# Mixer chains of a hybrid mLSTM and HGRN2 layer, their product groups spaced by the unit

## The chip, the cores and the metric

The kernel runs on one core of one Trainium2 chip. A core has TensorE (PE, matrix products into PSUM banks), VectorE (DVE), ScalarE (ACT), GpSimd (POOL) and SyncE (SP, which issues the DMAs). The metric is the time of one execution on the device in microseconds (us); lower is better.

## The reference

One decoder layer works on 1024 new prompt positions and 8 sequences of 4 sampled positions, 1056 columns in all. What matters here:

```python
p = jnp.einsum('btd,dp->btp', _rmsnorm(x, norm_mix), w_in) + b_in       # 1024 -> 4104
out_a = sigmoid(o) * headnorm(mlstm(silu(conv(qk)), v, i, f))           # 4 heads of 128
out_b = headnorm(hgrn(silu(q), f, i)) * silu(g)                         # 4 heads of 128
x = x + concat([out_a, out_b]) @ w_out
x = x + (silu(h2 @ w_gate) * (h2 @ w_up)) @ w_down
# mlstm: W = exp(D - m); num = w_inter * (q C) + ((q k) * W) v; C <- decay * C + sum(w_last k v)
# hgrn:  A = sum_k q k exp(b_t - b_s); o = (q exp(b)) S + A v; S <- exp(b_L) S + (k exp(b_L - b)) v
```

headnorm divides each head's row by the root of its mean square. The states C and S are outputs too.

## The kernel before, in words

All data lies transposed, features on the partitions and time along the columns. The 1056 columns are cut into three blocks b of 288, 384 and 384 (the first holds the 32 sampled columns). The in-projection takes one weight tile of 128 output features at a time; each **unit** is one weight tile times one block: eight k-tiles of three main matmuls each (L135 to L137: high part of x times high part of w, low times high, high times low). For a head h and a block b there are four units: q, k, v, o for the mLSTM heads (a), then f, q, v, g for the HGRN2 heads (b). After all heads comes the out-projection, again in units (264 columns), which needs all chains' outputs split into HI and LO (mix_split, L994 and L995).

The work between projections, the **mixer**, runs in Python generators: mix_a(h, b) and mix_b(h, b). A list of active chains is advanced by hook(), which is called after the second, fourth and sixth k-tile and after the end of each unit, so there are four **places** per unit and 16 per block of a head. At a place each active chain, oldest first, writes its next piece of instructions behind the main matmuls; yield n lets n places pass. So the queues of all engines are in the order in which hook() met the pieces, and the waits in the chains set which places share pieces. finish(key) calls hook() until a chain is done, at one place: that happens before the out-projection's unit needs a k-tile whose split isn't written.

A chain's pieces on PE: in mix_a scores, k transposed, v transposed (L528, L532, L535), state products (L551), output (L572, L574), and the output transposed (L590); in mix_b four groups of level products (L777 twice, then L855 and L860), v and k transposed (L874, L877), state products (L891), output (L911, L913), transposed output (L928). The numbers of places between them stand in MAW (L502, a row for h = 0 and each block, and one for all other heads) and, for mix_b, as constants in its yields. All of them write PSUM tiles of the tag mx, of which four rotate; main matmuls have three of the tag mm.

Between the groups other engines work: ACT squares the output (L580, L918), DVE and POOL take the root (norm_cols, L495 to L500), DVE multiplies by it (L585, L923), and after the transposes DVE multiplies by the gate (L592, L930) and writes the result to X, from where mix_split takes it. In mix_b DVE takes products into AD (L784), ACT copies them to AT (L846), and the steps (L796, L798, L804, ACT L801, L802) prepare q and k of the next level; AT times v is the output. The units' evacuations are ACT and DVE too: the HGRN2 gate by L743 to L746. A weight tile is split by ACT (L96) and by POOL (L97, 512 columns each). Sampled columns have a chain of their own (sample_core, L626 to L699), with state products L674 and L646 for each sequence.

Of the kernel before, what the change touches and what calls it, by code (L numbers as in the profile page):

```python
# [9 lines left out]
F32 = mybir.dt.float32  # L10
# [13 lines left out]
NB = 3  # L24
H = 4
# [15 lines left out]
def hybrid_step(ctx: ExitStack, tc: tile.TileContext, i, o):  # L41
# [6 lines left out]
    mp = p1.enter_context(tc.tile_pool(name="mixp", bufs=1))  # L48
# [3 lines left out]
    def bank(tag="mx"):  # L52
        return psum.tile([128, 512], F32, tag=tag, name=tag, bufs={"mm": 3, "mx": 4, "so": 1}[tag])
# [136 lines left out]

    def ntile(tag="nt"):
        if tag in ("raw", "W"):
            return mp.tile([128, 387], F32, tag=tag, name=tag, bufs=2 if tag == "raw" else 1)
        if tag == "na":
            return cn.tile([128, QN], F32, tag=tag, name=tag, bufs=1)
        return cn.tile([128, 384], F32, tag=tag, name=tag, bufs=2)
# [43 lines left out]
    def tl(tag, n=384, bufs=2, dt=F32, p=128):  # L240
        return mp.tile([p, n], dt, tag=tag, name=tag, bufs=bufs)
# [250 lines left out]
    def norm_cols(s, sqs, nch, d2=None, p=128):  # L492
# [14 lines left out]

    def mix_a(h, b):
        w = MAW[b if h == 0 else 3]
# [3 lines left out]
        while ("gc", b) not in done or ("cv", "k") not in done:  # L513
            yield 1
        ng, wi = S["ng", h, b], S["wi", h, b]
        W = mp.tile([128, 387], F32, tag="W", name="W", bufs=1)
        for c in range(ncb):
            s = slice(c * 128, c * 128 + 128)
            nc.vector.scalar_tensor_tensor(W[:, s], ng[:, s], cols[:, c0 + c, 0, h:h + 1], maskneg,
                                           op0=OP.add, op1=OP.add)  # L520
        nc.scalar.activation(W[:, :npr], W[:, :npr], AF.Exp)
        qw = tl("qw")
# [14 lines left out]
        if (h, b) == (0, 0):  # L537
            nc.gpsimd.memset(ktm, 0.0)
        kt = tl("kt", 384, 1)
# [5 lines left out]
                                cols[:, c0:c0 + ncb, 2, h:h + 1].to_broadcast([128, ncb, 128]), op=OP.mult)  # L545
        nc.vector.scalar_tensor_tensor(W[:, :npr], pS[:, :npr], QS, W[:, :npr], op0=OP.mult, op1=OP.mult)
        yield w[2]
# [22 lines left out]
        for c in range(ncb):  # L570
            s = slice(c * 128, c * 128 + 128)
            nc.tensor.matmul(pO[:, c, 0:129], W[:, s], vt[:, c, 0:129], start=True, stop=cin[c] is None)  # L572
            if cin[c] is not None:
                nc.tensor.matmul(pO[:, c, 0:129], qw[:, s], cin[c], start=False, stop=True)  # L574
        yield w[5]
        sm = mp.tile([128, 3, 4], F32, tag="sm", name="sm", bufs=2)
        hn = tl("kt", 384, 1)
        nc.scalar.activation(sm[:, 1, :ncb, None], pO[:, :ncb, 128:129], AF.Square)
        for c in range(ncb):
            nc.scalar.activation(hn[:, c * 128:c * 128 + 128], pO[:, c, 0:128], AF.Square, accum_out=sm[:, 0, c:c + 1])  # L580
# [121 lines left out]
    def sample_a():  # L702
# [12 lines left out]
        for h in range(H):  # L715
            nc.tensor.matmul(pS[32 * h:32 * h + 32, 0:32], kS[:, h, :], qS[:, h, :], start=True, stop=True,
                             tile_position=(0, 32 * h))
        W = tl("sW", 32, 1)
        nc.vector.scalar_tensor_tensor(W, ngS, scol[:, 0:1], mneg4, op0=OP.add, op1=OP.add)
# [29 lines left out]
    def mix_b(h, b):  # L749
# [2 lines left out]
        AT, AD = ATs[atn[0] % 2], ADs[atn[0] % 2]  # L752
        atn[0] += 1
        samp = b == 0
        gx = tl("wib", 388, 2)
        qp = tl("qw")

# [32 lines left out]
        def step(lv, src, dst):  # L790

            nn = n if samp and lv <= 2 else npr
            G, go = gst
            nb = nn // (2 * lv)
            gv = G[:, go:go + nn // lv].rearrange("p (n two) -> p n two", two=2)
            nc.vector.tensor_tensor(odd(dst[0][:, :nn], lv), odd(src[0][:, :nn], lv), gv[:, :, 0:1].to_broadcast([128, nb, lv]),  # L796
                                    op=OP.mult)
            nc.vector.tensor_tensor(even(dst[1][:, :nn], lv), even(src[1][:, :nn], lv), gv[:, :, 1:2].to_broadcast([128, nb, lv]),  # L798
                                    op=OP.mult)
            if dst is not src:  # L800
                nc.scalar.activation(even(dst[0][:, :nn], lv), even(src[0][:, :nn], lv), AF.Copy)  # L801
                nc.scalar.activation(odd(dst[1][:, :nn], lv), odd(src[1][:, :nn], lv), AF.Copy)  # L802
            go2 = 0 if lv == 1 else go + nn // lv
            nc.vector.tensor_tensor(gx[:, go2:go2 + nb, None], gv[:, :, 0:1], gv[:, :, 1:2], op=OP.mult)  # L804
            gst[:] = gx, go2
# [59 lines left out]
            nc.scalar.activation(AT[s0:s0 + 32, :ncb, s0 + 32:s0 + 64], pc[s0:s0 + 32], AF.Copy)  # L865
        nc.scalar.activation(AT[0:64, :ncb, 64:128], ps[0:64, 128:128 + 64 * ncb].rearrange("p (c t) -> p c t", t=64), AF.Copy)
        step(64, B, B)
        yield 1
        go, qp, k = gst[1], qB, kB
        v = S["vb", h, b]  # L870
        pK, pV = bank(), bank()
# [7 lines left out]
        kt = tl("kt", 384, 1)  # L879
# [3 lines left out]
        if samp:  # L883
            nc.gpsimd.tensor_copy(ss_["sv"][:, h, :], v[:, 256:288])
            nc.gpsimd.tensor_copy(ss_["so"][:, h, :], S["g", h, b][:, 256:288])
        yield 2
        pU = bank()
        C = mp.tile([128, 3, 130], F32, tag="C", name="C", bufs=2)
        for c in range(ncb):
# [14 lines left out]
        Sst[h] = prev  # L904
        if b == 2:
            nc.sync.dma_start(o["Sp"][h], prev)
        yield 2
        pO = bank()
        for c in range(ncb):
            s = slice(c * 128, c * 128 + 128)  # L910
# [2 lines left out]
                nc.tensor.matmul(pO[:, s], qp[:, s], cin[c], start=False, stop=True)  # L913
        yield 1
        sm = mp.tile([128, 3, 4], F32, tag="sm", name="sm", bufs=2)
        hn = tl("kt", 384, 1)
        for c in range(ncb):
            nc.scalar.activation(hn[:, c * 128:c * 128 + 128], pO[:, c * 128:c * 128 + 128], AF.Square,  # L918
                                 accum_out=sm[:, 0, c:c + 1])
# [1 line left out]
        yield 2  # L921
        for c in range(ncb):
            nc.vector.tensor_scalar_mul(hn[:, c * 128:c * 128 + 128], pO[:, c * 128:c * 128 + 128], sm[:, 2, c:c + 1])  # L923
        yield 6
        pH = bank()
        for c in range(ncb):
            s = slice(c * 128, c * 128 + 128)
# [23 lines left out]
    for h in range(H):  # L951
        ts = [wtile(wa[1 + 4 * h + j]) for j in range(4)]
        for b in range(NB):
            gu = len(units) + (1 if b else 0)
            evs = [conv_evac("q", h, b), conv_evac("k", h, b),
                   act_evac("v", "v", AF.Identity, V_BIN + 8 + h, h, b),
                   act_evac("o", "go", AF.Sigmoid, V_BIN + 12 + h, h, b, 2)]
            posts = [(lambda h, b: lambda: load_bc(h, b))(h, b) if h else None, None,
                     spawn((lambda h, b: lambda: mix_a(h, b))(h, b), "a", h, b), None]
            if h == H - 1 and b == 0:  # L960
                posts[3] = spawn(sample_a, "sa")
            in_group(ts, b, evs, posts, (("mm", "mm", "mx", "mx") if (h, b) == (0, 0) else None))
            if h == 0:
                unit(tg, hrhs(b), KT, gates_evac(b))
                units.insert(gu, units.pop())
# [43 lines left out]
    def out_evac(m, q):  # L1009
        def ev(ps):  # L1010
            x = xq(q)
            nc.vector.tensor_tensor(x[:, m, :], x[:, m, :], ps[:, :QN], op=OP.add)
            dst = ntile(("raw", "raw", "W", "na")[q]) if m == 0 else ntile()
            nc.scalar.activation(dst[:, :QN], x[:, m, :], AF.Square)
            if m == 0:
                naccs[q] = dst
            else:
                nc.vector.tensor_tensor(naccs[q][:, :QN], naccs[q][:, :QN], dst[:, :QN], op=OP.add)
            if m in (4, KT - 1):
                s = slice(0, 5) if m == 4 else slice(5, KT)  # L1020
                nc.sync.dma_start(d_x[:, s, q * QN:(q + 1) * QN], x[:, s, :])
            if m == KT - 1:
                start(norm2(q), ("n2", q))
        return ev
# [945 lines left out]
```

## Time and profile before

| what | value |
|---|---|
| time, median of 3 runs | 1389.78 us (1387.84 to 1392.84) |
| the profiled execution | 1390.61 us |
| its span, first to last instruction | 1388.5 us |
| PE busy | 1339.8 us, 96% |
| DVE, ACT, POOL busy | 865.7, 558.1, 595.9 us |
| mean granted clock of TensorE | 0.979 |

The profile lists busy time by engine, the waits of an instruction with the engine and tile that released it, and instructions in order of time. A matmul's listed duration overlaps the next one's, so the spacing of starts tells what one costs. In-projection and mixers fill the time to about 563 us, the out-projection follows, then the feed-forward network.

### The profile page before, as it was taken

Reading aid. Unit: us, or ns where it says so; the run is one execution under the profiler, and the core shown is the slowest. Engines: PE = TensorE matmul, PEld = TensorE weight load, DVE = VectorE, ACT = ScalarE, POOL = GpSimd, SP = SyncE. Lnnn points to the kernel's source line nnn. Section 1 sums busy time; section 2 is a strip of 40 time slices with the busy share of each in tenths; the row PEclk is TensorE's granted clock in tenths of the full one; section 3 lists DMA queues with packets and bytes.
Section 4 is the critical chain, followed back from the end, with each engine's and each line's share of the span. In section 5 each row is a group of like instructions: output and inputs, shape, how many; then the busy total and the mean of one; then the engine's idle time right before and its main releaser. Section 6 shows DMA issues by size and latency. Waiting matters only on the chain. (4 is left out here: it accounts for less than half of the span.)

```text
span 1388.5 us, 29405 instructions
## 1 busy us (share of the span) xinstructions
PE 1339.8 (96%) x11600; PEld 1309.3 (94%) x11600; DVE 865.7 (62%) x2060; ACT 558.1 (40%) x1315; POOL 595.9 (43%) x566
## 2 busy tenths in 40 slices
PE   7988999999999999999999999999999999999996
PEld 6878999899999998899999999999999999999995
DVE  6876667664545456644675667666665347777765
ACT  5554434233444344422435445554544342122232
POOL 5323212231222223222547666666666684444434
PEclk9989999999999999999999999999999999999997
DMA  6012222230111113553455566566664279878733
GB/s 227 23 30 66 66 67 74 80 117 17 49 32 34 47 49 117 150 161 126 163 187 178 205 228 242 207 221 251 213 221 168 79 255 354 300 276 298 271 137 125
DMA packets 109937, 212.12 MB, mean 153 GB/s; under 512 B 11088, under 2 KB 63848, under 8 KB 109288
## 3 DMA queue, kind: packets, MB, share of 16 engines
q1 hardware_dynamic: 109368, 209.98, 43.8%
q8 instruction: 91, 1.49, 0.4%
q14 instruction: 46, 0.38, 0.1%
q10 hardware_dynamic: 432, 0.27, 0.1%
HBM read 143.76 MB, written 66.45 MB: 151 GB/s over the span
## 5 line engine op out<-in xcount | busy, mean ns | idle before, releaser
L135 PE MATMUL mm<-HI,whi 128*128 128x384 f32 (+2 forms) x1160 | 380.3, 328 | 5.3 <-ACT gA L304 2.9
L137 PE MATMUL mm<-HI,wlo 128*128 128x384 f32 (+2 forms) x1160 | 364.5, 314 | 0.9 <-POOL wlo L97 0.8
L136 PE MATMUL mm<-LO,whi 128*128 128x384 f32 (+2 forms) x1160 | 364.2, 314 | 0.2 <-DVE LO L225 0.2
L135 PEld LDWEIGHTS mm<-HI,whi 128*128 128x128 f32 x1160 | 222.3, 192 | 10.4 <-ACT gA L304 3.2
L137 PEld LDWEIGHTS mm<-HI,wlo 128*128 128x128 f32 x1160 | 222.1, 191 | 1.4 <-POOL wlo L97 1.4
L136 PEld LDWEIGHTS mm<-LO,whi 128*128 128x128 f32 x1160 | 222.4, 192 | 0.8 <-DVE LO L225 0.5
L97 POOL TENSOR_TENSOR wlo<-raw,whi 128x512 fp32r<-128x512 f32 x90 | 118.7, 1329 | 216.5 <-ACT whi L96 171.5
L1199 POOL TENSOR_TENSOR wlo<-S,whi 128x512 fp32r<-128x512 f32 x78 | 111.0, 1430 | 87.5 <-ACT whi L1198 84.6
L1270 PE MATMUL mx<-T,whi 128*128 128x264 f32 x640 | 118.3, 284 | 0.0
L1270 PEld LDWEIGHTS mx<-T,whi 128*128 128x128 f32 x640 | 99.2, 188 | 0.0
L1323 POOL TENSOR_TENSOR LO<-rg,HI 128x528 fp32r<-128x528 f32 x52 | 70.6, 1368 | 64.2 <-ACT HI L1322 64.1
L1270 PE MATMUL mx<-HI,whi 128*128 128x264 f32 x320 | 91.0, 284 | 0.0
L1270 PE MATMUL mx<-T,wlo 128*128 128x264 f32 x320 | 90.9, 284 | 0.0
L1270 PE MATMUL mx<-HI,wlo 128*128 128x264 f32 x320 | 90.9, 284 | 0.0
L1270 PE MATMUL mx<-LO,whi 128*128 128x264 f32 x320 | 90.7, 283 | 0.0
L1411 DVE TENSOR_TENSOR fh<-fr,fh 128x512 fp32r<-128x512 f32 x80 | 66.9, 837 | 32.4 <-ACT fh L1406 32.1
L1497 DVE TENSOR_TENSOR X<-X,mx 128x264 f32<-128x264 f32 x160 | 65.6, 424 | 28.1 <-PE mx L1493 27.6
L1198 ACT ACTIVATE whi<-S 128x512 fp32r<-128x512 f32 x80 | 50.3, 630 | 68.1 <-DVE S L1187 67.9
L1322 ACT ACTIVATE HI<-rg 128x528 fp32r<-128x528 f32 x52 | 32.3, 641 | 104.3 <-PE mx L1493 29.5
L1270 PE MATMUL mm<-HI,whi 128*128 128x264 f32 x240 | 68.3, 284 | 1.1 <-ACT nt L1054 1.1
L1270 PE MATMUL mm<-HI,wlo 128*128 128x264 f32 x240 | 68.2, 284 | 0.0
L1270 PE MATMUL mm<-LO,whi 128*128 128x264 f32 x240 | 67.9, 283 | 0.0
(545 smaller groups left out, 3421.6 us busy)
## 6 DMA issues: line engine op xcount, KB each, us to landing
d_wf<-fh SPq DMA_DIRECT2D x60, 512.0 KB
rg<-d_ff SPq DMA_DIRECT2D x42, 528.0 KB
raw<-in_wA SPq DMA_DIRECT2D x31, 512.0 KB
whi<-d_wf SPq DMA_DIRECT2D x29, 512.0 KB
wlo<-d_wf SPq DMA_DIRECT2D x28, 512.0 KB
raw<-in_wgu SPq DMA_DIRECT2D x24, 512.0 KB
d_ff<-sg SPq DMA_DIRECT2D x40, 264.0 KB
rg<-in_wgu SPq DMA_DIRECT2D x20, 512.0 KB
```

Source lines behind the costliest of these rows:

```text
L97: (nc.gpsimd if pool else nc.vector).tensor_tensor(lo[:, s], raw[:, s], hi[:, s].bitcast(F32), op=OP.subtract)
L135: nc.tensor.matmul(ps[:, :n], wh, rh[:, k, :], start=(k == 0), stop=False)
L136: nc.tensor.matmul(ps[:, :n], wh, rl[:, k, :], start=False, stop=False)
L137: nc.tensor.matmul(ps[:, :n], wl, rh[:, k, :], start=False, stop=(k == nk - 1))
L1198: nc.scalar.activation(hi[:, s], t, AF.Copy)
L1199: (nc.vector if dve else nc.gpsimd).tensor_tensor(lo[:, s], t, hi[:, s].bitcast(F32), op=OP.subtract)
L1270: nc.tensor.matmul(ps[:, :QN], a[:, w], b_[:, kk, c], start=new and kk == 0 and x == 0, stop=kk == 3 and x == 2, skip_group_check=True)
L1322: nc.scalar.activation(h, src, AF.Copy)
L1323: (nc.vector if dve else nc.gpsimd).tensor_tensor(lw, src, h.bitcast(F32), op=OP.subtract)
L1411: nc.vector.tensor_tensor(lw, src, h.bitcast(F32), op=OP.subtract)
L1497: nc.vector.tensor_tensor(y, y, ps[:, :QN], op=OP.add)
```

## The change

The row of MAW for the heads 1 to 3 of mix_a gets other numbers: the output (before at place 9 of the chain) comes at place 18, its multiply at 21 instead of 13, the transposes at 34 instead of 19, the last multiply at 35 instead of 20; scores, transposes and state products stay at 2 and 6. In mix_b four waits become w, (3, 3, 3, 5) for all but the last block of the last head, which keeps (1, 2, 2, 6): v and k transposed at place 18 (before 16), state products at 22 (19), output at 26 (22), transposed output at 34 (31); the level products stay at 2, 6, 10 and 14. As the groups are then apart by whole units, each place that holds a group holds one of the next two blocks' too. The squares get a tile hn instead of sharing kt, and W two buffers instead of one. No instruction is added or taken away.

```diff
-            return mp.tile([128, 387], F32, tag=tag, name=tag, bufs=2 if tag == "raw" else 1)
+            return mp.tile([128, 387], F32, tag=tag, name=tag, bufs=2)
...
-        (2, 1, 3, 1, 2, 2, 2, 6, 1))
+        (2, 1, 3, 1, 11, 1, 2, 13, 1))
...
-        W = mp.tile([128, 387], F32, tag="W", name="W", bufs=1)
+        W = mp.tile([128, 387], F32, tag="W", name="W", bufs=2)
...
-        hn = tl("kt", 384, 1)
+        hn = tl("hn", 384, 1)
...
+        w = (1, 2, 2, 6) if (h, b) == (H - 1, NB - 1) else (3, 3, 3, 5)
...
         step(64, B, B)
-        yield 1
+        yield w[0]
...
             nc.gpsimd.tensor_copy(ss_["so"][:, h, :], S["g", h, b][:, 256:288])
-        yield 2
+        yield w[1]
...
             nc.sync.dma_start(o["Sp"][h], prev)
-        yield 2
+        yield w[2]
...
             nc.vector.tensor_scalar_mul(hn[:, c * 128:c * 128 + 128], pO[:, c * 128:c * 128 + 128], sm[:, 2, c:c + 1])
-        yield 6
+        yield w[3]
```

What it does on PE in a steady stretch of the HGRN2 heads, before (main matmuls between the groups are left out; mx is the product's PSUM tile, AT the taken products, cq, qw, qB the three forms of q and ck, kB of k):

```order
L855 MATMUL mx<-qw,ck 32x32 x6
L860 MATMUL mx<-qB,kB 32x64 x6
...
L928 MATMUL mx<-ident,kt 128x128 x3
...
L874 MATMUL mx<-ident,v 128x128 x3
L877 MATMUL mx<-ident,kB 128x128 x3
...
L777 MATMUL mx<-cq,ck 32x32 x9
L777 MATMUL mx<-qw,ck 32x16 x9
...
L891 MATMUL mx<-vt,kt 128x128 x3
```

The same stretch after (line numbers behind the change are one higher):

```order
L856 MATMUL mx<-qw,ck 32x32 x6
L861 MATMUL mx<-qB,kB 32x64 x6
...
L929 MATMUL mx<-ident,hn 128x128 x3
L875 MATMUL mx<-ident,v 128x128 x3
L878 MATMUL mx<-ident,kB 128x128 x3
L778 MATMUL mx<-cq,ck 32x32 x9
L778 MATMUL mx<-qw,ck 32x16 x9
...
L892 MATMUL mx<-vt,kt 128x128 x3
L778 MATMUL mx<-qw,ck 32x16 x9
L778 MATMUL mx<-qB,kB 32x16 x8
```

Transposed output of one block, transposes of the next and the first level products of the one after it stand together, and state products with the second level products; between such places lie 24 main matmuls.

PE in the last mLSTM head, head 3, its last block, before (cq, ck are q and k, W the weights, C the state, kt what is transposed to the output):

```order
L528 MATMUL mx<-cq,ck 128x128 x3
L532 MATMUL mx<-ident,ck 128x128 x3
L535 MATMUL mx<-ident,v 128x128 x3
...
L590 MATMUL mx<-ident,kt 128x128 x3
...
L551 MATMUL mx<-vt,kt 128x129 x3
...
L572 MATMUL mx<-vt,W 128x129
L574 MATMUL mx<-C,qw 128x129
```

And after: the place at which the third block's scores stand (hn is the squares' tile, now the scaled output):

```order
L590 MATMUL mx<-ident,hn 128x128 x2
L572 MATMUL mx<-vt,W 128x129
L574 MATMUL mx<-C,qw 128x129
...
L528 MATMUL mx<-cq,ck 128x128 x3
L532 MATMUL mx<-ident,ck 128x128 x3
L535 MATMUL mx<-ident,v 128x128 x3
```

Before, the output and its transposes stood at places of their own, one and two units apart. After, five PSUM tiles of mx are written there in a row.

DVE where the out-projection begins, before (LO, HI: the split input; L1012 adds a finished unit to X; smx, st: the sample's result and state):

```order
L995 TENSOR_TENSOR LO_80<-X_78,HI_79 128x496
L930 SCALAR_TENSOR_TENSOR X_78<-mx_6932,vec_74,go_6354 128x384
L693 TENSOR_SCALAR sjunk_6898<-so_6418,sm_6897 128x128
L995 TENSOR_TENSOR LO_80<-X_78,HI_79 128x528
L662 TENSOR_SCALAR svm_6964<-svt_6412,cst_76 128x128
L882 COPY kt_6974<-mx_6956 128x384
L1012 TENSOR_TENSOR X_78<-X_78,mm_6779 128x264
L699 SCALAR_TENSOR_TENSOR smx_81<-mx_6972,vec_74,so_115 128x32 x4
```

and after:

```order
L996 TENSOR_TENSOR LO_80<-X_78,HI_79 128x496
L693 TENSOR_SCALAR sjunk_6898<-so_6410,sm_6897 128x128
L662 TENSOR_SCALAR svm_6955<-svt_6404,cst_76 128x128
L883 COPY kt_6965<-mx_6947 128x384
L699 SCALAR_TENSOR_TENSOR smx_81<-mx_6963,vec_74,so_115 128x32 x4
L931 SCALAR_TENSOR_TENSOR X_78<-mx_6972,vec_74,go_6344 128x384
L996 TENSOR_TENSOR LO_80<-X_78,HI_79 128x528
L902 SCALAR_TENSOR_TENSOR C_6982<-C_6693,wib_6551,mx_6981 128x128
L902 SCALAR_TENSOR_TENSOR C_6982<-C_6982,wib_6551,mx_6981 128x128 x2
L651 SCALAR_TENSOR_TENSOR st_6918<-st_6918,gS_124,mx_6986 128x128 x2
L651 SCALAR_TENSOR_TENSOR st_6918<-st_6918,gS_124,mx_6987 128x128 x2
L1013 TENSOR_TENSOR X_78<-X_78,mm_6765 128x264
```

The last multiply of the block before the last, with the last LO part of k-tile 7 that hangs on it, moved behind the sample's result, and the first addition of an out-projection unit behind the state updates.

## Rows read from the trace of the kernel before

**Rows 1.** Busy time by windows of 50 us: window, its length, then busy us of each engine (instructions), granted clock of TensorE, share of the DMA engines and GB/s.

```profile
350.00:400.00 50.00, 49.69 (x671) 47.15 (x669) 26.55 (x99) 18.77 (x63) 12.45 (x13) 1.00 0.14 45
...
550.00:600.00 50.00, 47.96 (x501) 45.48 (x500) 29.94 (x94) 18.15 (x53) 9.53 (x14) 1.00 0.52 154
```

**Rows 2.** What PE waited for between 135 and 700 us: us in total, times, longest.

```profile
PE mx L860 <- DVE wib L804: 4.0, 5, 2.0
PE mx L574 <- DVE C L559: 1.6, 1, 1.6
```

**Rows 3.** Timeline of PE around three single groups (two transposes, six transposes, level products): start us, duration, engine, line, operation, output and inputs, shapes, count.

```profile
411.05 0.34 PE L137 MATMUL mm<-HI,wlo 128*128 128x384 f32 x1
411.22 0.38 PE L928 MATMUL mx<-ident,kt 128*128 128x128 f32 x2
...
411.62 0.34 PE L136 MATMUL mm<-LO,whi 128*128 128x384 f32 x1
...
412.32 0.34 PE L137 MATMUL mm<-HI,wlo 128*128 128x384 f32 x1
...
413.33 0.34 PE L136 MATMUL mm<-LO,whi 128*128 128x384 f32 x1
...
415.06 0.34 PE L137 MATMUL mm<-HI,wlo 128*128 128x384 f32 x1
...
416.16 0.34 PE L136 MATMUL mm<-LO,whi 128*128 128x384 f32 x1
```

**Rows 4.** The same around an output group of six matmuls alone (mLSTM).

```profile
214.14 0.34 PE L137 MATMUL mm<-HI,wlo 128*128 128x384 f32 x1
214.31 0.38 PE L572 MATMUL mx<-vt,W 128*128 128x129 f32 x2
...
215.83 0.34 PE L136 MATMUL mm<-LO,whi 128*128 128x384 f32 x1
```

**Rows 5.** The same around an output group of six and level products in one place (HGRN2; the level products, L777, stand at the end of the lines left out).

```profile
420.70 0.34 PE L137 MATMUL mm<-HI,wlo 128*128 128x384 f32 x1
420.88 0.38 PE L911 MATMUL mx<-vt,AT 128*128 128x128 f32 x2
...
423.12 0.33 PE L136 MATMUL mm<-LO,whi 128*128 128x384 f32 x1
```

**Rows 6.** Timeline at the first block of mLSTM head 3; in brackets the idle time before and what ended it.

```profile
252.53 0.32 DVE L636 TENSOR_SCALAR svm<-svt,cst 128x129 f32<-128x129 f32 x1
...
253.24 0.49 PE L574 MATMUL mx<-C,qw 128*128 128x129 f32 x2 [1.58 <-DVE C L559]
```

**Rows 7.** Timeline at the first HGRN2 chain, POOL, DVE and PE.

```profile
317.96 1.41 POOL L97 TENSOR_TENSOR wlo<-raw,whi 128x512 fp32r<-128x512 f32 x1 [8.48 <-ACT whi L96]
318.15 1.36 DVE L798 TENSOR_TENSOR ck<-kB,wib 128x128 f32<-128x128 f32 x1
...
319.66 0.32 PE L777 MATMUL mx<-qw,ck 128*32 128x16 f32 x16 [0.89 <-DVE wib L804]
```

**Rows 8.** Timeline at step32 of a chain whose next block has 384 columns.

```profile
407.42 0.58 ACT L743 ACTIVATE ngb<-mm,vec 128x384 f32<-128x384 f32 x1 [0.64 <-PE mm L137]
...
409.11 0.35 DVE L798 TENSOR_TENSOR kB<-ck,wib 128x192 f32<-128x192 f32 x1
...
409.57 1.28 POOL L97 TENSOR_TENSOR wlo<-raw,whi 128x512 fp32r<-128x512 f32 x1 [8.21 <-ACT whi L96]
409.61 0.53 PE L860 MATMUL mx<-qB,kB 128*32 128x64 f32 x12
```

**Rows 9.** The same where the next block has 288 columns: the scaling by the norm (DVE), and the step32 products (PE).

```profile
363.41 0.86 DVE L923 TENSOR_SCALAR kt<-mx,sm 128x128 f32<-128x128 f32 x3
...
367.83 0.53 PE L860 MATMUL mx<-qB,kB 128*32 128x64 f32 x12 [0.20 <-DVE wib L804]
```

**Rows 10.** The squares on ACT between 300 and 560 us, grouped by line: count, busy us, mean ns of one, idle time before.

```profile
L918 ACT ACTIVATE kt<-mx 128x128 f32<-128x128 f32 x29 | 7.7, 274 | 20.0 <-PE mx L913 20.0
```

**Rows 11.** Timeline where the out-projection begins.

```profile
568.89 0.49 PE L928 MATMUL mx<-ident,kt 128*128 128x128 f32 x3
...
570.09 0.60 DVE L930 SCALAR_TENSOR_TENSOR X<-mx,vec,go 128x384 f32<-128x384 f32 x1
...
570.73 0.65 ACT L994 ACTIVATE HI<-X 128x528 fp32r<-128x528 f32 x1 [1.60 <-DVE X L930]
...
571.40 0.71 DVE L995 TENSOR_TENSOR LO<-X,HI 128x528 fp32r<-128x528 f32 x1 [0.45 <-ACT HI L994]
...
571.80 0.28 PE L135 MATMUL mm<-HI,whi 128*128 128x264 f32 x1
...
572.17 0.39 PE L136 MATMUL mm<-LO,whi 128*128 128x264 f32 x1
...
572.92 0.91 PE L891 MATMUL mx<-vt,kt 128*128 128x128 f32 x6
...
573.66 1.06 PE L646 MATMUL mx<-svm,ktm 128*128 128x128 f32 x8
...
577.42 1.12 DVE L651 SCALAR_TENSOR_TENSOR st<-st,gS,mx 128x128 f32<-128x128 f32 x4
```

**Rows 12.** Timeline at step32 of the last chain but one, beside the splits of the out-projection's input.

```profile
538.48 1.17 ACT L994 ACTIVATE HI<-X 128x528 fp32r<-128x528 f32 x2
...
539.28 0.53 PE L860 MATMUL mx<-qB,kB 128*32 128x64 f32 x12 [1.41 <-DVE wib L804]
```

More of the change, by code (lines that the diff above doesn't have):

```diff
@@ L915, in mix_b @@
         sm = mp.tile([128, 3, 4], F32, tag="sm", name="sm", bufs=2)
-        hn = tl("kt", 384, 1)
+        hn = tl("hn", 384, 1)
         for c in range(ncb):
```

## The prediction

> **What bounds the kernel now.** I read the busy windows first, then the waits of TensorE (PE), then the timeline around those waits. Between 135 and 700 us the end is set by PE: in the window 350 to 400 us it is busy 49.69 of 50 us at a granted clock of 1.00, and in 550 to 600 us, where the in-projection ends and the out-projection begins, 47.96 us, again at 1.00 [rows 1]. So a microsecond is won only if PE needs less time for its instructions or waits less. What it waits for is short: in these 565 us the step32 products wait five times for VectorE (DVE), 4.0 us together, and an output group once 1.6 us [rows 2]; level products wait once 0.89 us [rows 7]. Those waits are the whole pool that a better spacing could empty, some 6.5 us of 1390. The other half of the question is what a group of products costs besides its own matmuls, because the change makes about 50 groups fewer by putting several in one place.
>
> **Fewer groups.** A group's price is the time from the main matmul before it to the second one after it, less two main slots of 0.17 us (0.17 is one row's step, 411.05 to 411.22). Two transposes alone cost 411.62 - 411.05 - 0.34 = 0.23 us and six cost 413.33 - 412.32 - 0.34 = 0.67, three times as much: 0.11 each and no fixed part. A level group of 24 + 24 small products 416.16 - 415.06 - 0.34 = 0.76 us [rows 3]. An output group of six alone costs 215.83 - 214.14 - 0.34 = 1.35 us [rows 4]. The kernel before already has six output matmuls and 24 + 24 small products in one place: 423.12 - 420.70 - 0.34 = 2.08 us [rows 5]. The sum of the two apart is 2.11. Merging saved 0.03 us, less than two roundings. With 50 merges at 0 (as transposes say) to 0.012 (something under half of that 0.03, which is little more than the rounding of the rows) the term is 0 to -0.6; I take **-0.3 us**. No group gets more or fewer matmuls.
>
> **The sample's stall, head 3, block 0.** One group waits 1.58 us at 253.24 for the state C [rows 6]. That output group now comes 9 places later, so this wait is gone. But the sample's products of the same place read svm, which DVE delivers at 252.53 + 0.32 = 252.85 [rows 6], and PE would stand there from about 251.5. What is late next is thus almost as late: 0 to -1.6, taken **-0.3 us**.
>
> **The stall at 319.66.** Level-16 products wait 0.89 us, because DVE's product of 1.36 us (318.15) runs beside GpSimd's (POOL) 1.41 us split [rows 7]; ahead of both in DVE's queue stands the last multiply of an mLSTM block, which now is issued a place earlier. 0 to -0.9, taken **-0.6 us**, since the queue is shorter by one such multiply (0.60 us is its like in [rows 11]).
>
> **Place 14 of the HGRN2 chains.** The output group (1.35 us) now stands in place 10 in front of the level products, and ScalarE (ACT) then has three squares of 0.274 us, 0.8 together [rows 10] and with their accumulator reads an estimated 0.9, before DVE's norm step and the takes. The squares can run while PE does the level products (0.76), so the takes come about 0.9 + 0.2 + 0.2 - 0.76 = 0.5 us later against the products than if nothing stood there. In the kernel before, three multiplies of 0.86 us (363.41) stood there instead [rows 9]; they move behind step32. In blocks of 384 columns ACT has 0.64 us free before the next gate's sigmoid (407.42), and that sigmoid, not the takes, times step32 [rows 8]: the cover is larger than the 0.5, so nothing. If that cover were gone, each block would lose up to 0.5. After block 2 the next block has 288 columns and no such cover: step32's products wait 0.20 there already [rows 9]. Three such chains at +0.15 (from -0.2, the wait goes, to +0.5): **+0.45 us**, bounds -0.6 to +1.5.
>
> **The merged mLSTM group.** In one place now stand: transposed output of block n-2, output group of n-1, then scores, k and v transposes of n. That is five banks of a rotation of four, so the v transposes wait until DVE has read the first bank (0.60 us for such a multiply [rows 11]). Queued behind the waiting transposes is everything on PE. The cover is what lies between: 1.35 [rows 4] plus nine matmuls for scores and k, at 0.11 about 1 us. 0.6 plus a DVE queue of up to 1.5 fits nearly always; once or twice DVE beside POOL is slow, as at 318.15 [rows 7]. 0 to 1.5, taken **+0.3 us**. vt, kt and W: kt no longer is shared with the squares' output hn and W has a second buffer, so the later output waits for no buffer: 0.
>
> **The junction with the out-projection.** This is the largest term. The last but one HGRN2 block now ends three places later, and its transposed output falls into the hooks that are forced just before k-tile 7 of the first out-projection units. Before, transposes at 568.89 let DVE multiply at 570.09, ACT write HI at 570.73, DVE write LO until 572.11, with fifteen mains and more in between; PE still lost 0.37 - 0.12 = 0.25 at 572.17 (0.12 is a main of 264 columns, 0.17 x 264 / 384) [rows 11]. Now, from the start of the transposes: 0.49 for them, 0.60, 0.65 and 0.71 for the three steps, and 0.04 + 0.04 + 0.02 + 0.06 between them, 2.61 us until k-tile 7's LO matmul [rows 11]. PE has the transposes 0.33, the state products 573.66 - 572.92 = 0.74, the sample's products 8 x 0.11 = 0.88 and one main: 2.07. Wait 0.54, so +0.3 net. Behind that on DVE stand three state updates (about 1.1), four of the sample (1.12 us [rows 11]) and the add (0.4) that frees the first bank: 2.55 + 2.62 = 5.2 against PE's 2.61 + 5 x 0.12 + 1.35 + 0.36 = 4.9 at the fourth unit, +0.3. Step32 of the last chain has squares and norm in front, as above: +0.3. And the multiplies (three, 0.86 as in [rows 9]) now stand in DVE's queue before its last steps, whose k is transposed next: 0 to 0.86, taken 0.6. Sum **+1.5 us**, bounds 0.5 (little more than the first alone) to 3 (each term doubled).
>
> **The stall at 539.28.** 1.41 us behind DVE's and ACT's backlog of the splits of the out-projection's input [rows 12]. PE now arrives later there by an output group of three matmuls (half of 1.35), and two multiplies go out of the queue ahead: 0 to -1.2, taken **-0.7 us**.
>
> Sum: -0.3 - 0.3 - 0.6 + 0.45 + 0.3 + 1.5 - 0.7 = +0.35 us. On the profiled execution of 1390.61 (span 1388.5 and 2.1 around it) this is 1391.0; that execution lies 0.83 above the median of 1389.78, and against the median it is **1390.1 us**. The lower ends of all terms add to -4.4, the upper ones to +6.0: 1385.4 to 1395.8.
>
> **Rivals.** *All waits go.* If the even spacing lets DVE be early everywhere, the 6.5 us of [rows 2] vanish and the junction keeps its place: 1383.3 or, with the junction's 1.5, 1384.8. For it: DVE is the waited-for engine in every row. Against: three of the five step32 waits lie at the end, where the splits and not the spacing make DVE late [rows 11, 12]. Chance 0.08. *Groups have a price of their own.* If each left group saved 0.1, 50 x 0.1 = 5 us, 1384.8; [rows 5] speaks against it. Chance 0.03.
>
> *Step32 runs into POOL (slower).* In 384-column blocks DVE's second product of step32 ends at 409.46, POOL's split begins at 409.57, and PE takes the result at 409.61 [rows 8]: the margin is 0.11 to 0.15. If the squares and the norm pass on more than ACT's 0.64, DVE's last products of step32 start after POOL's and take 1.36, as at 318.15 [rows 7], instead of 0.35. The price is 1 us in each of eight chains, 8 us, less the covered ones: some 6 to 8 us, 1396 to 1398. It decides once the takes come later than by 0.64 us. Against: my 0.5. Chance 0.14. The Trainium skill ("SBUF — State Buffer", section on the two separate sides) says that DVE with two SBUF inputs and GpSimd share a port pair under an exclusive lock, and that the loser blocks for the whole instruction. The rows at 318.15 agree: DVE's product ends at 319.51, 0.14 after POOL's at 319.37 [rows 7]. By that rule a step32 that starts only just after POOL would wait out the 1.28 us of 409.57, and the sum for all eight chains would be an estimated 8 x (1.28 - 0.15) = 9.0 instead of +0.35.
>
> *The change does nothing that PE can see*: merged groups cost the sum, waits move about and cancel, junction hidden: 1389.8, chance 0.15, within the forecast's range.
>
> **How the numbers follow.** Forecast 0.60, no effect 0.15, waits gone 0.08, price of groups 0.03, POOL 0.14. A measurement tells 0.3%, 4.2 us, from no change. Forecast and no effect lie within it but for a small tail: same 0.74. Faster: 0.08 + 0.03 - what stays above 1385.6 = 0.10 with the forecast's tail. Slower: 0.14 + 0.02 = 0.16. The range takes in the bounds of the terms but for their joint ends and leaves out most of the two outer cases: 1386 to 1395.5.
>
> **What would show it.** In the profile after: groups of five kinds of products in one place that cost their sums (0.33 + 1.35 + 12 x 0.11 = 3.0 us where an mLSTM chain has its five [rows 3, 4]); no wait of the output group at 253 but one of the sample's products there; new waits of k-tile 7 near 572 and of the transposes ahead; step32 in 384-column blocks still without a wait. I am wrong if a steady block of 384 columns changes its length by more than 0.3 us either way, or if the granted clock falls below 1.00 between 150 and 700 us.

## The result, and the profile after

The changed kernel takes 1392.42 us (median of 20 runs, 1390.01 to 1396.93), the kernel before in the same comparison 1390.39 (20 runs, 1386.99 to 1392.84): a ratio of 1.002, 95% interval 1.0013 to 1.0028. That is some 2 to 3 us slower, within the 0.3% that were called no change, but clear of zero. The forecast was +0.35.

Single executions also differ where the change moves nothing: in the fourteen traces of this study the main matmul that begins at 137.95 us before begins between 136.38 and 138.38, and what follows the one at 715.44 takes 668.8 to 673.7 us. So traces are compared over a stretch. The main matmul that begins at 137.95 us in the trace before and the one that begins at 614.08 are 476.13 us apart. In the trace after the same two begin at 137.36 and 616.90: 479.54, so **+3.41 us**. From the end of the mLSTM chains (338.58) to the same phase three HGRN2 heads later (529.58), steady repetition, it is +1.14. The waits of PE between 135 and 700 us after (engine, tile, line, releaser: us in total, times, longest), beside [rows 2]:

```profile
PE mx L861 <- DVE wib L805: 4.4, 8, 0.8
PE so L674 <- DMA st<-in_C: 1.6, 1, 1.6
PE so L674 <- DMA st<-in_S: 1.5, 1, 1.5
PE mx L535 <- DVE X L592: 1.4, 2, 0.7
PE mx L646 <- DVE svm L636: 1.2, 1, 1.2
PE mx L207 <- DVE W L1019: 1.2, 1, 1.2
PE mm L135 <- DVE X L1013: 0.7, 2, 0.4
PE mx L696 <- DVE sjunk L693: 0.6, 1, 0.6
PE mm L136 <- DVE LO L996: 0.4, 1, 0.4
PE mx L878 <- DVE wib L805: 0.3, 1, 0.3
```

The output group's wait for C and the level products' 0.89 are gone. Step32 (L861) waits eight times instead of five, but never longer than 0.8. New are the v transposes (L535), svm, the sample's state by in_C, and at the junction with the out-projection the k transposes (L878), k-tile 7 (L136) and a unit that waits for the add (the second of L1013). The wait for in_S was there before and grew from 0.4 to 1.5.

A merged place, timeline of PE at a block of 288 columns: transposes, output of six, scores, k and v of two chunks, then mains:

```profile
184.73 0.30 PE L137 MATMUL mm<-HI,wlo 128*128 128x288 f32 x1
184.86 0.49 PE L590 MATMUL mx<-ident,hn 128*128 128x128 f32 x3
...
187.55 0.29 PE L136 MATMUL mm<-LO,whi 128*128 128x288 f32 x1
```

187.55 - 184.73 less two slots of 0.13 is 2.56 us; the parts are 3 x 0.11 + 1.35 [rows 4] + 8 x 0.11 = 2.56. Merging saved nothing.

The same kind of place where PE waits, all engines, and at the end the weight operations of a place where PE does not wait:

```profile
166.63 2.91 DVE L519 SCALAR_TENSOR_TENSOR W<-ngb,cols,cst 128x128 f32<-128x128 f32 x3
166.72 2.67 POOL L97 TENSOR_TENSOR wlo<-raw,whi 128x512 fp32r<-128x512 f32 x2 [2.94 <-ACT whi L96]
169.93 0.47 DVE L592 SCALAR_TENSOR_TENSOR X<-mx,vec,go 128x256 f32<-128x256 f32 x1
170.55 0.52 PE L535 MATMUL mx<-ident,v 128*128 128x128 f32 x3 [0.73 <-DVE X L592]
...
202.23 0.87 DVE L519 SCALAR_TENSOR_TENSOR W<-ngb,cols,cst 128x128 f32<-128x128 f32 x3
```

L592 frees the bank that L535 needs. It stands in DVE's queue behind the three weight operations, which take 2.91 us here beside two splits of POOL, and 0.87 at 202.23. Of the seven merged places the two that wait are the two where they take 2.91.

Step32 of a chain of block 0, all engines; before, the same L743 began at 385.64 and step32's products at 388.00 without a wait:

```profile
384.18 0.28 ACT L919 ACTIVATE hn<-mx 128x128 f32<-128x128 f32 x1 [2.01 <-PE mx L914]
...
385.10 0.17 DVE L495 TENSOR_SCALAR sm<-sm 128x3 f32<-128x3 f32 x1 [2.81 <-ACT hn L919]
385.18 0.41 DVE L785 COPY_PREDICATED AD<-msk,mx 128x32 f32<-128x32 uint8 x2
385.62 1.05 ACT L847 ACTIVATE AT<-AD 32x64 f32<-32x64 f32 x4 [0.55 <-DVE AD L785]
386.68 0.63 ACT L96 ACTIVATE whi<-raw 128x512 fp32r<-128x512 f32 x1
387.22 0.57 ACT L743 ACTIVATE ngb<-mm,vec 128x384 f32<-128x384 f32 x1
387.39 1.28 POOL L97 TENSOR_TENSOR wlo<-raw,whi 128x512 fp32r<-128x512 f32 x1 [1.13 <-ACT whi L96]
387.82 1.07 DVE L745 TENSOR_SCALAR ngb<-ngb,omlb,lb 128x384 f32<-128x384 f32 x1 [1.75 <-ACT ngb L743]
...
389.77 0.42 PE L861 MATMUL mx<-qB,kB 128*32 128x64 f32 x8 [0.64 <-DVE wib L805]
```

The reader is to follow it downwards: squares, norm step, takes, AT copies, weight split, and only then the gate's sigmoid, with no free time on ACT from 385.62 on. POOL's split then lies beside DVE's L745. This chain has nothing of the 0.64 us of cover that [rows 8] show.

The sample's states: the new wait behind head 3, and the one at the end, where two loads of X stand ahead of the fetch in SP's queue (SPq). The first begins as DVE's split of 540.57 ends; the second takes 1.44 us to issue (0.46 at 544.73, and why is not shown).

```profile
253.90 1.16 PE L646 MATMUL mx<-svm,ktm 128*128 128x129 f32 x8 [1.24 <-DVE svm L636]
...
266.48 0.43 PE L674 MATMUL so<-st,qz 128*32 128x129 f32 x8 [1.64 <-DMA st<-in_C]
...
540.57 0.71 DVE L996 TENSOR_TENSOR LO<-X,HI 128x528 fp32r<-128x528 f32 x1
541.30 0.37 SPq L981 DMA_DIRECT2D X<-in_xT  x1
541.72 1.44 SPq L982 DMA_DIRECT2D X<-in_xT  x1
543.26 0.40 SPq L610 DMA_DIRECT2D st<-in_S  x1
546.67 0.43 PE L674 MATMUL so<-st,qz 128*32 128x128 f32 x8 [1.52 <-DMA st<-in_S]
```

### The profile page after: what moved, and what is told of

Same layout as the page of the kernel before. It is cut to its first block, busy times and chain, and to the rows that moved or that the text cites. A ratio compares the mean times of both kernels' runs of the same rounds, so it can differ in the third digit from the quotient of the medians.

```text
span 1390.7 us, 29414 instructions
## 1 busy us (share of the span) xinstructions
PE 1334.7 (96%) x11600; PEld 1304.8 (94%) x11600; DVE 871.6 (63%) x2060; ACT 560.1 (40%) x1315; POOL 595.2 (43%) x566
## 5 line engine op out<-in xcount | busy, mean ns | idle before, releaser
L135 PE MATMUL mm<-HI,whi 128*128 128x384 f32 (+2 forms) x1160 | 374.9, 323 | 7.0 <-ACT gA L304 2.9
L136 PE MATMUL mm<-LO,whi 128*128 128x384 f32 (+2 forms) x1160 | 362.6, 313 | 0.7 <-DVE LO L996 0.4
L136 PEld LDWEIGHTS mm<-LO,whi 128*128 128x128 f32 x1160 | 221.1, 191 | 1.7 <-DVE LO L996 0.6
L500 POOL TENSOR_TENSOR sm<-sm,mhalf 128x3 f32<-128x3 f32 (+2 forms) x26 | 21.3, 818 | 145.4 <-DVE AD L785 65.8
```

The lines of the kernel that those rows point to most:

```text
L135: nc.tensor.matmul(ps[:, :n], wh, rh[:, k, :], start=(k == 0), stop=False)
L136: nc.tensor.matmul(ps[:, :n], wh, rl[:, k, :], start=False, stop=False)
```

## The experiments

Each is timed against the kernel before (ratio with its 95% interval). "Stretch" is the time from the main matmul at 137.95 to that at 614.08, "heads" that from 338.58 to 529.58 (starts in the trace before), both less the trace before. The waits are those of the lists, in us (with how often); "state" is the DMA's, the first by in_C and the second by in_S.

| kernel | ratio | stretch | heads | step32 | L535 | svm | state |
|---|---|---|---|---|---|---|---|
| before | 1 | 0 | 0 | 4.0 (5) | 0 | 0 | 0, 0.4 |
| the change | 1.0020 (1.0013 to 1.0028) | +3.41 | +1.14 | 4.4 (8) | 1.4 (2) | 1.2 | 1.6, 1.5 |
| mLSTM alone | 1.0017 (1.0004 to 1.0030) | +1.50 | -0.35 | 4.0 (5) | 1.4 (2) | 1.1 | 1.4, 0.8 |
| HGRN2 alone | 1.0013 (1.0000 to 1.0026) | +1.16 | +1.14 | 4.4 (8) | 0 | 0 | 0, 1.7 |
| squares late | 0.9995 (0.9982 to 1.0008) | +2.10 | -1.62 | 0.9 (2) | 1.4 (2) | 1.2 | 1.6, 1.8 |
| transposes early | 1.0013 (1.0001 to 1.0024) | +1.70 | +1.23 | 4.4 (8) | 0 | 1.3 | 0.9, 1.6 |
| multiplies late | 1.0000 (0.9988 to 1.0012) | +1.32 | +1.12 | 5.3 (9) | 0 | 0.5 | 0.9, 1.6 |
| junction as before | 1.0020 (1.0007 to 1.0034) | +3.20 | +1.23 | 5.6 (8) | 1.4 (2) | 1.3 | 1.5, 0 |
| loads later | 1.0013 (1.0002 to 1.0024) | +1.80 | +1.28 | 4.4 (8) | 1.4 (2) | 1.3 | 1.3, 0 |
| three cures | 0.9978 (0.9969 to 0.9988) | -3.03 | -1.44 | 2.0 (3) | 0 | 0.5 | 0.8, 0 |
| four | 0.9961 (0.9948 to 0.9974) | -3.52 | -1.39 | 1.1 (2) | 0 | 0.5 | 1.1, 0 |
| own places | 1.0036 (1.0023 to 1.0050) | +4.84 | +1.48 | 5.4 (8) | 1.4 (2) | 1.2 | 1.1, 1.6 |
| buffers alone | 0.9983 (0.9972 to 0.9995) | -0.25 | -0.43 | 4.0 (5) | 0 | 0 | 0, 0.9 |
| before, again | 0.9996 (0.9984 to 1.0008) | +2.28 | -0.20 | 4.0 (5) | 0 | 0 | 0, 0.9 |

Two of these stretches, of squares late and of the kernel before run again, hold some 1.5 us of a lowered clock (see there).

The theory after the result: groups cost their sum wherever they stand, and the loss is waits for DVE and DMA that the new places bring. The rival: places have a price, or the loss is the junction.

**One half at a time.** The change without the new waits of mix_b, and without the new row of MAW:

```diff
-        w = (1, 2, 2, 6) if (h, b) == (H - 1, NB - 1) else (3, 3, 3, 5)
+        w = (1, 2, 2, 6)
```
```diff
-        (2, 1, 3, 1, 11, 1, 2, 13, 1))
+        (2, 1, 3, 1, 2, 2, 2, 6, 1))
```

> The change for the mLSTM chains alone; the HGRN2 chains keep their old waits (tiles hn and W as in the change). Theory (two prices, one in each half): the v transposes of the merged mLSTM place wait for DVE twice, 0.7 us each in the waits and 0.9 each in what the place costs; the sample's stall at head 3 goes on as a wait for svm and then for the DMA of its state; the level-16 wait of 0.89 at 319 is gone; step32 products wait as before, 0.2 in the chains of block 2 and nothing in those of block 0. In all +1 to +2 us against the kernel before. Rival (the loss is all in the HGRN2 half): no wait of the v transposes worth 0.3, and a time at or below the kernel before.

> The change for the HGRN2 chains alone; the mLSTM heads 1 to 3 keep their old places. Theory: step32 products wait 0.65 us in each of three chains of block 0 and 0.45 in those of block 2, per head +0.4 us against the kernel before after what the level products of block 2 no longer wait; the v transposes of mLSTM wait nowhere; the output group of head 3 waits 1.6 us for C again. In all +0.5 to +1.5 us against the kernel before. Rival (the loss is all in the mLSTM half): 0 or less.

Both came as the theory said: +1.50 and +1.16, each half with its own waits and none of the other's. Both rivals fall, though the times alone hardly tell it: the interval of the second begins at 1.0000. The halves add to 2.66, the change has 3.41; the rest is not explained, and two traces of the kernel before differ by as much without the clock (2.28 - 1.5).

**The squares of HGRN2.**

```diff
-        w = (1, 2, 2, 6) if (h, b) == (H - 1, NB - 1) else (3, 3, 3, 5)
+        w = (1, 2, 2, 6, 1) if (h, b) == (H - 1, NB - 1) else (3, 3, 3, 3, 3)
...
-        yield 1
+        yield w[4]
```

> The change with the squares of the HGRN2 output, their norm and the multiply two places later (squares at place 29, behind step32's copies, multiply at 31, transposes at 34 as in the change). Theory (the three squares on ACT push the AT copies, the weight split and the next gate's sigmoid, and so step32): the waits of 0.65 and 0.45 fall to 0 to 0.2 each, in all -2 to -2.7 us against the change. Rival (POOL's weight split beside DVE's gate arithmetic is the cause, the squares only happen to be there): waits of 0.5 or more stay in the chains of block 0. Second rival: the squares now push something else, and the waits move to the k transposes or to the level products: no gain.

In the three heads -1.62 instead of +1.14, so -2.76; the waits of step32 are down to two, both at the end. The same chain as above:

```profile
386.36 1.29 POOL L97 TENSOR_TENSOR wlo<-raw,whi 128x512 fp32r<-128x512 f32 x1 [3.31 <-ACT whi L96]
386.37 0.58 ACT L743 ACTIVATE ngb<-mm,vec 128x384 f32<-128x384 f32 x1
...
388.74 0.42 PE L861 MATMUL mx<-qB,kB 128*32 128x64 f32 x8
```

POOL's split lies beside the gate here too, and step32 waits for nothing: the squares, with the norm step and the multiply that moved with them, are the cause; both rivals fall in the heads.

Over the whole stretch the gain is 1.31 only, but the rest is no price of the edit: in this trace the granted clock fell after the wait for in_S (1.80 us, up to 544.16). Windows of 3 us, columns as in [rows 1]:

```profile
544.00:547.00 3.00, 2.84 (x17) 2.57 (x18) 0.89 (x3) 0.00 (x0) 2.16 (x4) 0.60 1.02 298
547.00:550.00 3.00, 3.00 (x61) 2.58 (x60) 2.11 (x6) 1.01 (x2) 1.78 (x4) 0.83 0.54 183
```

Main matmuls step by 0.32 us there instead of 0.17, and the transposed output's place at 546 costs 2.46 instead of 1.62. Against the change these 3 us lose 1.6 beside the wait; without that the gain over the stretch would be an estimated 2.9. The cures below keep head 3's squares where the change has them; whether that was needed was not tested.

**The bank of the merged place.** Transposes at 31:

```diff
-        (2, 1, 3, 1, 11, 1, 2, 13, 1))
+        (2, 1, 3, 1, 11, 1, 2, 10, 1))
```

> The change with the mLSTM output transposed at place 31 instead of 34 and its last multiply at 32, so that DVE reads the bank before the next block's weights are prepared and the merged place writes four banks. Theory (bank wait behind DVE's queue): no wait of the v transposes, -1.4 to -1.8 us against the change, and the extra group costs nothing. Rival (a group has a price of its own, 0.1 us): 7 more groups, +0.7, so -0.7 to -1.1. Second rival (DVE is simply late there): the wait moves to the next reader of a bank, no gain.

L535 waits no more (the seven places cost their sums) and the state's DMA less, 0.9 for 1.6: -2.46 against the change up to 338.58, with seven more groups. Over the stretch it is -1.71, since in the out-projection a unit waits 0.6 longer for the add (L1013). The rival of a price per group fails here.

**The multiply ahead of svm.**

```diff
-        (2, 1, 3, 1, 11, 1, 2, 13, 1))
+        (2, 1, 3, 1, 11, 1, 5, 7, 1))
```

> The change with the mLSTM multiply by the norm at place 24 instead of 21, the transposes at 31 and the last multiply at 32. Theory (at head 3, block 0, three multiplies of 0.87 us stand in DVE's queue ahead of the sample's svm, and a later state update makes the next state's DMA late): besides the waits of the v transposes that go with place 31, the sample's wait for svm falls from 1.2 to 0.4 us or less and the wait for the state's DMA from 1.6 to below 0.5; -2.5 to -4 us against the change up to 333 us. Rival (the DMA itself is late, whatever DVE does): the wait for the state grows by what the wait for svm loses.

svm 1.2 to 0.5, where 0.4 or less was expected; the state 0.9, as already in the run before, not below 0.5: in this trace the three multiplies (from 256.03) now stand right ahead of the state's update (257.00). The rival's trade, state up by what svm loses, did not come either. Up to 338.58 it is 2.4 us below the change, a little short, because a ninth step32 wait of 0.9 came: the last mLSTM block's multiply at 24 meets the first HGRN2 chain. The transposes alone had gained 2.46 there, so the later multiply itself won nothing: what it saved at svm it lost at that step32.

**The junction and the loads.** The last two chains with the old waits; and the loads of X two splits later:

```diff
-        w = (1, 2, 2, 6) if (h, b) == (H - 1, NB - 1) else (3, 3, 3, 5)
+        w = (1, 2, 2, 6) if (h, b) >= (H - 1, 1) else (3, 3, 3, 5)
```
```diff
-            if m % 2:
+            if m % 2 and m > 1:
+                x_rows(m - 2, th)
+            if m == KT - 1:
                 x_rows(m, th)
```

> The change with the old waits for the last two HGRN2 chains instead of the last one, so that no transposed output falls into the forced hooks before k-tile 7 of the out-projection. Theory (the new waits at the junction are made up for by the stall of step32 that shrank there): the waits of k-tile 7 (0.4 in the list, 0.54 by the spacing) and of the k transposes (0.3) go, the step32 wait of the last chain returns from 0.8 towards the 2.0 of the kernel before, in all within 0.5 us of the change. Rival (the junction is the largest loss, as predicted): -1.5 us against the change with the last chain's step32 still at 0.8.

> The change with the loads of X for the out-projection issued two splits later (each after its split is long done), which changes nothing else. Theory (on SP's queue the sample's state fetch stands behind such a load, and that waits for DVE's split, which a POOL split beside it makes slow): the wait of the sample's products for the state near 545 falls from 1.5 to 0.4 or less, -1 us against the change. Rival (the fetch waits for its buffer or takes that long): unchanged 1.5.

With the junction as before, k-tile 7's wait is gone and step32 of the last chain waits 2.0 again: +3.20 against +3.41, within the 0.5 us of the theory. It is not the kernel before, though: the k transposes of the last but one chain wait 1.6 (at 546.63), where none was expected, and the wait for in_S is gone. With the loads later the wait for in_S is gone too, and the stretch is 1.61 shorter, of which 0.4 lie ahead of 338.58 and so ahead of the edit; level products wait 0.5 for POOL in its place. The fetch was issued at 538.33 instead of 543.26: it was late because it stood behind loads in SP's queue. That POOL made the split slow, as expected there, is not shown: the split of 540.57 took 0.71.

**Together.** Squares late for the heads 0 to 2, multiplies late, loads later; then the last mLSTM block with a row of its own, (2, 1, 3, 1, 11, 1, 2, 10, 1).

> The change with the three cures together: mLSTM multiply at 24 and transposes at 31, squares of HGRN2 two places later for the heads 0 to 2 (head 3 as in the change), loads of X two splits later. Theory: the gains add, about -2.5 to -4 up to 333 us, -2 to -2.5 from there to 535, -1 behind it: 5 to 7 us below the change and 3 to 4 below the kernel before, since the waits that the kernel before had at 319 and in the level products of block 2 stay gone. Rival (each cure only passes its wait on): no less than the kernel before.

> The three cures together, but with the last mLSTM block's multiply at place 21 as in the change, since at 24 it stands in DVE's queue ahead of step32 of the first HGRN2 chain (a wait of 0.8 there in the run with the three cures). Theory: that wait goes, -0.8 us against the three cures up to 333 us and nothing behind it; about 3.5 to 4 us below the kernel before. Rival: DVE is late there for another reason (the gate's arithmetic beside POOL's split) and the wait stays.

The gains add: -6.44 against the change in the stretch, where 5 to 7 was expected, and -6.93 with the fourth; 1387.05 us (0.9978 of the kernel before) and 1385.52 (0.9961). The fourth takes away the ninth step32 wait, but the one for in_C grows by 0.2, so it is 0.5 and not 0.8 below the three. Both are faster than the kernel before and than the change; that four is faster than three the times don't show, their intervals overlap. The buffers alone, which are in both, came out at 0.9983 (below), so a part of the 0.4% may be theirs; over the stretch the buffers have -0.25 and the four cures -3.52.

**Own places again, and the buffers.**

```diff
-        w = (1, 2, 2, 6) if (h, b) == (H - 1, NB - 1) else (3, 3, 3, 5)
+        w = (1, 2, 2, 6) if (h, b) == (H - 1, NB - 1) else (3, 4, 2, 4)
```

> The change with HGRN2's state products at place 23 instead of 22 and its transposed output at 33 instead of 34, so that some 20 groups of the steady stretch stand at places of their own again; outputs, level products and step32 stay where the change has them. Theory (a group has no price of its own, the loss is the waits): from 333 to 535 us the same as the change within 0.3 us, with the same step32 waits. Rival (each group costs 0.1 us for the switch): +1.5 to +2 us in that stretch.

With 18 groups more the three heads take 0.34 longer than with the change, just over the 0.3 expected and far from the rival's 1.5 to 2, with the same step32 waits. Place by place nothing is lost: state products and level products cost 0.67 + 0.73 apart and 1.39 together. Two traces of the kernel before differ by 0.20 in these heads. Behind them it lost more: step32 near 541 and 570 waits 0.9 and 1.2 instead of 0.3 and 0.8, and k-tile 7 waits 0.9 for HI, which is the junction one place on.

> The kernel before with the tile hn and the second buffer of W alone, all places as before. Both theories: the same waits and the same stretch as before within 0.2 us; the time within the measurement's spread. If it differs, part of what is put down to the places belongs to the buffers.

The waits are the same but for in_S (0.9 for 0.4), and the stretch moves by -0.25. The time, 0.9983 with an interval that excludes 1, is lower than that explains. So the kernel before was run against itself:

> The kernel before itself, unchanged, timed against the kernel before, since the buffers alone came out 0.17% faster while the stretch from 138 to 614 us moved by 0.25 us only. Theory (the stretch tells the effect, the rest is the spread of the part ahead of it): the ratio lies within 0.1% of 1 but may miss it by about as much as its interval. Rival (the intervals are as wide as they should be and the buffers gain 2 us somewhere): the ratio is 1 within 0.05%.

0.9996, with 1 well inside the interval. Where the buffers' further gain of perhaps 2 us lies, and whether it is one, stays open; both traces have the same order outside the stretch. If it is real, the new places cost that much more than the change as a whole. The stretch of this second trace is 2.28 us longer than the first's, of which 1.5 are the clock (below), 0.5 a longer wait for in_S and 0.3 a wait of the sample's products for POOL: a stretch tells 1 us only where its waits and its clock are looked at too.

## Why the prediction held, and where its sum was off

The time lies in the range and the forecast of no change above 0.3% was right; the sum was 2 to 3 us too low. That it held is in part luck: terms that came out lower than forecast (junction, 319, 539) miss by some 2 us, and terms that came out higher (place 14, the merged group, the sample's stall, a wait that was not in the sum) by more than 5. By its steps, with the costs of places worked out from spacings as there:

- **Fewer groups**, -0.3: the mechanism, that groups have no price of their own, was right. No saving shows; the merged places cost their sums within 0.02.
- **Place 14**, +0.45: mis-sized, and this is half the loss. Block 2 came near (1.48 against 1.24 us for step32's place, 0.25 each, given back by level products at place 10 that no longer stall, 2.06 against 1.34 + 0.94). The failed step is "in blocks of 384 columns ACT has 0.64 us free": it was read from one chain of block 1 and taken for all. In the chains of block 0 a weight split stands in front of the sigmoid and ACT has nothing free: waits of 0.65 us, and a place of 1.50 instead of 0.93, in each of three chains, 1.7 together. The rival of the later step32 had the cause half right (squares passing on more than the cover); its collision with POOL at step32 itself did not come.
- **The merged mLSTM group**, +0.3, at most 1.5: right mechanism, too small. Two of seven places waited, 3.80 us against 2.89 for the same work at 294: 0.9 each, 1.8.
- **The sample's stall**, -0.3: the wait did pass to svm, 1.2 for 1.6. The step that failed is that nothing was followed behind it: the state's update ended 1.0 us later (259.18 for 258.19), the next fetch went out 1.35 later, and PE waited 1.64 for it.
- **319**, -0.6: -1.08 (0.58 against 1.66 for the place), beyond its bound of -0.9.
- **539**, -0.7: 1.38 against 2.45, -1.07, as expected; but the state's wait at 545 rose from 0.4 to 1.5. It was not in the sum, since SP's queue behind the splits was not looked at. Of this, 0.5 also comes in the kernel before run again.
- **The junction**, +1.5: its parts came (k transposes +0.5; k-tile 7 waits 0.5, of which the kernel before had 0.25; the unit behind the add +0.6), but step32 of the last chain, put at +0.3, went from 2.99 to 1.85 for its place. As at 539, an output group now stands ahead of that chain's level products and the multiplies have moved behind step32, so DVE has worked off its queue when the takes come; with the old waits it is 2.99 again (the junction as before). Together +0.3. The largest term of the sum was thus wrong, and the loss lies in terms that it had small, with the wrong sign or not at all.

Two of the prediction's own signs came out against it. Step32 in blocks of 384 columns was to be without a wait. And no steady block of 384 columns was to change by more than 0.3 us: the blocks that begin at 380.67 and 402.30 before go from 21.63 to 22.79 and from 22.75 to 21.97. Groups that moved from one block into the next are part of both; the pair is 0.4 longer. The argument against "all waits go" also holds a misreading: two and not three of the five step32 waits lie at the end, 3.4 of the 4.0 us.

## What to carry to other kernels

Moving product groups into shared places won nothing on TensorE: a shared place cost the sum of its groups. A place that already holds two groups tells this before the change, as in [rows 5]. Two sizes of one kind are not enough: the level groups of 32 and 48 small products cost 0.58 and 0.74, which looks like a fixed part of 0.26, and yet output and level products cost 0.66 + 0.74 apart and 1.40 together. What the move changes is the queues of the other engines: follow every piece of a moved step (squares, norm, multiply, DMA) to what stands behind it in its queue, in each block shape and phase, since cover seen in one chain is not cover in the next. The cures were cheap once the waits were named: together with the buffers 0.4% below the kernel before, with no instruction taken away.

## What the runs showed that was not expected

After a wait of PE of 1.2 us near 673 us, present in every trace, the granted clock stayed at 1.00 in some executions and fell to 0.50 (1.2 of 2.4 GHz) in others. Windows of 2 us of the kernel with the transposes early; columns as in [rows 1]:

```profile
672.00:674.00 2.00, 0.83 (x7) 0.64 (x6) 1.18 (x3) 0.85 (x3) 2.00 (x2) 1.00 0.44 161
674.00:676.00 2.00, 2.00 (x15) 1.96 (x15) 0.76 (x4) 1.53 (x2) 1.22 (x2) 0.73 0.70 245
676.00:678.00 2.00, 2.00 (x11) 2.00 (x11) 0.00 (x0) 0.04 (x1) 0.15 (x1) 0.50 0.00 0
678.00:680.00 2.00, 2.00 (x15) 1.81 (x15) 0.70 (x2) 0.53 (x2) 0.00 (x0) 0.92 0.00 0
```

and of the changed kernel at the same work:

```profile
674.00:676.00 2.00, 0.82 (x8) 0.64 (x6) 1.27 (x3) 0.85 (x3) 2.00 (x2) 1.00 0.40 145
676.00:678.00 2.00, 2.00 (x18) 1.96 (x19) 0.76 (x4) 1.62 (x2) 1.22 (x2) 1.00 0.75 261
```

The same PE wait and busy share, 18 matmuls in the next 2 us against 15, and the part from the main at 614.08 to the one at 715.44 takes 102.89 us instead of 101.39. It fell there in four of the fourteen traces (transposes early, multiplies late, three cures, four). In the second trace of the kernel before it fell after the wait of 1.6 us at 253 (0.63 and 0.80 in windows of 3 us), 1.5 us again, and with the squares late after the one of 1.8 us at 544, 1.6 us. What decides is not shown here. So a wait of a little over a microsecond can cost as much again, two executions of one kernel can differ by it, and a loss that only one trace shows is to be read beside its clock.
